# A recorded and list-scheduled instruction order in a two-layer GDN/GLA decoder trunk

## The chip, the core and the metric

The kernel runs on one core of a Trainium2 chip. TensorE (PE in the profile) multiplies matrices into PSUM, VectorE (DVE), ScalarE (ACT) and GpSimd (POOL) do the elementwise work, and SyncE (SP) starts most transfers between HBM and the on-chip memory SBUF. Each engine works through its own list of instructions in a fixed order; an instruction waits at the head of its list until the semaphores that it names are high enough, and nothing behind it on that engine can pass. The metric is device time in microseconds (us) of one execution.

## What is computed

Two layers over 2048 tokens of width 1024, in float32. Layer 0 is a gated DeltaNet (GDN) with 8 heads, layer 1 is gated linear attention (GLA) with 4 heads; head keys have 128 channels, values 256.

```python
def reference(x, ...):
    for i in range(2):
        y = gdn_mixer(x, ...) if i == 0 else gla_mixer(x, ...)
        x = layer_norm(DEEP_ALPHA * x + y, ln_g[i], ln_b[i])
    return x
# a mixer: p = x @ w_in -> q, k, v, gate (and per-token decay logits)
# GDN: short causal conv + silu on q, k, v; S_t = exp(g) S (I - beta k k^T) + beta v k^T; o = S q
# GLA: S_t = diag(exp(gk_t)) S + k^T v; o = q S
# both: o * rms(o) * norm_w * silu(gate), then @ w_out
```

## The kernel before

The work is cut into 48 units: a unit is one head (`h`) of one group of 512 tokens (`gi`) in one layer (`kind`). `PHASES` sets the order of the groups: GDN 0, GDN 1, GLA 0, GDN 2, GLA 1, GDN 3, GLA 2, GLA 3; a GDN group has 8 units, a GLA group 4. Inside a unit there are four threads of work:

- `gemms`: three input projections (`kq`, `val`, `gate`). Each runs over 8 chunks of 128 rows of the weight. A chunk of the weight is loaded to `wraw`, rounded by ACT to `wh`, and POOL writes the rest `wl = wraw - wh`; the input is split likewise into `xh` and `xl` (`load_x`, ACT and DVE). A float32 product is then three passes in the faster type fp32r (`mm3`: hi*hi, hi*lo, lo*hi). The sums stand in the PSUM banks `psg` (three of them).
- `preps`: the within-chunk matrices. For GDN (`gdn_prep`) this holds a triangular inverse: its diagonal blocks `X` go to HBM (`blk`) and come back replicated (`Arep`), then DVE solves 15 steps in turn (`Xt`, `X`), and PE and DVE widen the inverse (`Tm`, `U`, `W2`) to `Uf`, written over `D1`.
- `chains`: the recurrence over 4 chunks of 128 tokens. In GDN a chunk is `kq`*`S` (PE, into `psh`), `Rt` (DVE), `Uf`*`Rt` (PE), `wt` (ACT copy), `kd`*`wt` (PE), `S` (DVE): three round trips from PE and back, one `psh` bank. Then `og` is transposed and split to `oth`, `otl`.
- `outs`: the output projection, 8 pairs (token tile, half of the width) of a unit, each a *group* of 6 matmuls into `pso`, of which there is one bank, and one DVE instruction that adds it to `y` (`y<-pso,z,y`). The bank is free for the next group when that instruction is done. After the last head of a group comes the LayerNorm.

All 48 units are unrolled. The order on the engines comes about in two steps. The threads are Python generators; `Plan` keeps a rough clock of the engines (`COST`), and `plan.run` always continues the first thread whose operands should be there (chains, preps, outs, gemms, in that order). `O_GAP` keeps two output groups 7050 ns apart on that clock, `Y_WAIT` holds the first `y` load back, `W.load` starts weight loads `W_BUFS` = 9 chunks ahead. The order in which instructions are emitted is their urgency for the scheduler of the language's tile layer, which then sets the order on each engine by its own model, and places the tiles in their buffers. Every recorded operation carries line L121, so the rows below are told apart by their tiles.

## Time and profile before

| | |
|---|---|
| time, median of 3 runs | 3254.07 us (3253.61 to 3254.88) |
| span of the profiled execution | 3246.0 us, 55989 instructions |
| busy: PE, DVE, ACT, POOL | 3064.1, 2466.0, 1565.6, 1127.2 us |
| DMA over the span | 299.83 MB, mean 92 GB/s |
| median less span | 8.07 us |

The span runs from the first to the last instruction in the profile; the median of the runs is 8.07 us more, which lies around it. A row of a timeline reads: start, duration, engine, line, operation, output<-inputs, sizes, count, and in brackets the idle time before it and what ended it. A matmul's record is longer than the distance to the next one, since matmuls overlap in the array: a row of many merged matmuls gives the true distance. In float32 a matmul is two records, and in fp32r one.

### The profile page before, as it was taken

The page shows a single profiled execution, that of the slowest core. Times are in us where ns is not written, and L with a number is a line of the kernel's source. Part 1 is how long each engine was busy: PE and PEld are TensorE (multiplying, and loading weights), DVE is VectorE, ACT ScalarE, POOL GpSimd, SP SyncE. Part 2 cuts the span into 40 slices and gives each one's busy share as a digit, 9 for nine tenths or more (in the row PEclk, how much of TensorE's full clock was granted, in tenths as well). Part 3 has the DMA queues.
Part 4 walks back from the last instruction along what each step waited for, and adds up shares of the span by engine and source line. Part 5 has one row for each costly group of instructions (what it writes and reads, how often), then busy time and mean ns, then how long its engine had stood idle before and what let it go on. Part 6 is the DMA issues. An engine that isn't in the chain of part 4 may idle for free.

```text
span 3246.0 us, 55989 instructions
## 1 busy us (share of the span) xinstructions
PE 3064.1 (94%) x18430; PEld 2601.6 (80%) x18430; DVE 2466.0 (76%) x6345; ACT 1565.6 (48%) x4099; POOL 1127.2 (35%) x1506
## 2 busy tenths in 40 slices
PE   8899999989999999998999999999899999899997
PEld 7688778768888888877887888978778878798885
DVE  7677788787877687688778768677877786866677
ACT  5445444445444456444444545553444454465542
POOL 5333333333233234334233324432433322433341
PEclk9899999999999999999999999999999999999998
DMA  6222223242222315324222322532422232243231
GB/s 179 63 77 74 78 73 98 82 147 76 74 78 78 101 53 153 109 79 127 80 79 82 92 73 67 153 98 78 136 77 74 82 94 69 78 137 97 66 125 59
DMA packets 311604, 299.83 MB, mean 92 GB/s; under 512 B 40544, under 2 KB 253792, under 8 KB 311312
## 3 DMA queue, kind: packets, MB, share of 16 engines
q1 hardware_dynamic: 285200, 278.42, 30.0%
q10 hardware_dynamic: 26112, 17.83, 1.9%
q8 instruction: 145, 2.38, 0.3%
q14 instruction: 147, 1.20, 0.1%
HBM read 269.86 MB, written 26.28 MB: 91 GB/s over the span
## 4 chain that ended last, share of the span: by engine, by line
PE 47%; DVE 20%; DMA 7%; issue 2%; ACT 2%; POOL 0%; SPq 0%; DVEq 0%; ACTq 0%; POOLq 0%
PE psg L121 24%; PE psc L121 10%; PE pso L121 10%; DMA Arep<-blk 5%; PE psh L121 4%; DVE X L121 3%; DVE D L121 2%; DVE y L121 2%; DVE acc L121 2%; DVE Xt L121 2%; DVE lntmp L121 1%; DMA blk<-X 1%; DVE z L121 1%; DVE lnrs L121 1%; DVE lnst L121 1%
## 5 line engine op out<-in xcount | busy, mean ns | idle before, releaser
L121 POOL TENSOR_TENSOR wl<-wraw,wh 128x256 fp32r<-128x256 f32 x1152 | 950.0, 843 | 1349.7 <-ACT wh L121 1207.9
L121 ACT CAST wh<-wraw 128x256 fp32r<-128x256 f32 x1152 | 444.6, 405 | 373.9 <-PE psg L121 229.2
L121 PE MATMUL psg<-wh,xh 128*128 128x256 f32 (+1 forms) x2048 | 609.5, 298 | 12.8 <-ACT acc L121 6.1
L121 PE MATMUL psg<-wl,xh 128*128 128x256 f32 (+1 forms) x2048 | 586.4, 286 | 2.7 <-POOL wl L121 2.5
L121 PE MATMUL psg<-wh,xl 128*128 128x256 f32 (+1 forms) x2048 | 585.7, 286 | 0.0
L121 PE MATMUL psg<-xh,wh 128*128 128x512 f32 x1280 | 525.6, 411 | 2.9 <-DVE vt L121 1.3
L121 PE MATMUL psg<-xl,wh 128*128 128x512 f32 x1280 | 518.8, 405 | 0.6 <-DVE xl L121 0.6
L121 PE MATMUL psg<-xh,wl 128*128 128x512 f32 x1280 | 514.8, 402 | 0.1
L121 PEld LDWEIGHTS psg<-wh,xh 128*128 128x128 f32 x2048 | 392.6, 192 | 30.4 <-ACT acc L121 6.9
L121 PEld LDWEIGHTS psg<-wl,xh 128*128 128x128 f32 x2048 | 393.3, 192 | 16.5 <-POOL wl L121 3.8
L121 PEld LDWEIGHTS psg<-wh,xl 128*128 128x128 f32 x2048 | 392.9, 192 | 1.0
L121 PE MATMUL pso<-woh,oth 128*128 128x512 f32 x736 | 326.3, 443 | 61.7 <-DVE y L121 55.7
L121 DVE SCALAR_TENSOR_TENSOR acc<-pb,taps,acc 128x512 f32<-128x512 f32 x384 | 330.1, 862 | 44.4 <-ACT acc L121 39.1
L121 DVE SCALAR_TENSOR_TENSOR y<-pso,z,y 128x512 f32<-128x512 f32 x368 | 273.6, 743 | 111.7 <-PE pso L121 109.2
L121 PE MATMUL pso<-woh,otl 128*128 128x512 f32 x736 | 304.8, 414 | 12.9 <-DVE otl L121 11.5
L121 PE MATMUL pso<-wol,oth 128*128 128x512 f32 x736 | 298.6, 406 | 0.0
L121 PEld LDWEIGHTS psg<-xh,wh 128*128 128x128 f32 x1280 | 243.9, 191 | 56.1 <-DVE sg L121 3.2
L121 PEld LDWEIGHTS psg<-xh,wl 128*128 128x128 f32 x1280 | 242.7, 190 | 54.7 <-POOL wl L121 1.0
L121 PEld LDWEIGHTS psg<-xl,wh 128*128 128x128 f32 x1280 | 243.4, 190 | 53.4 <-DVE xl L121 2.5
L121 ACT ACTIVATE junk<-psc 128x128 bf16<-128x128 f32 (+1 forms) x448 | 144.2, 322 | 185.4 <-PE psc L121 150.8
L121 PEld LDWEIGHTS pso<-woh,oth 128*128 128x128 f32 x736 | 140.2, 190 | 100.9 <-DVE y L121 72.0
L121 DVE TENSOR_TENSOR Xt<-Arep,X 128x60 f32<-128x60 f32 (+14 forms) x480 | 131.9, 275 | 84.7 <-DMA Arep<-blk 76.6
(192 smaller groups left out, 5459.0 us busy)
## 6 DMA issues: line engine op xcount, KB each, us to landing
wraw<-in_w_in SPq DMA_DIRECT2D x1152, 128.0 KB, 2.3
woraw<-in_w_out SPq DMA_DIRECT2D x192, 256.0 KB, 3.6
Arep<-blk SPq DMA_DIRECT2D x32, 512.0 KB
woraw<-in_xT SPq DMA_DIRECT2D x32, 256.0 KB, 3.2
y<-in_x SPq DMA_DIRECT2D x16, 512.0 KB, 4.3
Gb<-gcT ACTq DMA_DIRECT2D x32, 256.0 KB, 3.0
x<-y SPq DMA_DIRECT2D x32, 256.0 KB, 2.1
x2T<-th ACTq DMA_DIRECT2D x32, 256.0 KB, 4.4
```

The source lines that it names most:

```text
L121: ins = op(*args, **kw)
```

## The change

The threads become plain functions, called for one unit after the other; nothing is emitted then. A `Recorder` notes each operation with its operands (`View`s of buffers that are not yet chosen), the operations that it depends on, a cost, and a rank: chains 0, preps 1, outs 2, gemms 3. `place` then runs a list schedule over five engines (DVE, ACT, POOL, PE, SP): the engine that can start soonest takes, of the operations whose operands and buffers are there, the one with the lowest rank, and within a rank the earlier one. It also gives a new tile the buffer that came free first. An operation that needs a new tile is held back while its unit is more than `HORIZON` = 2 units ahead of the oldest unit whose chain isn't finished. `emit` writes the operations in the order found, and ties each to the operation before it on its engine with an edge that carries no wait, so the tile layer's scheduler can't reorder them. The multiset of instructions is the same: 15921 matmuls, 1646 transfers on SP, and so on for each engine.

```diff
-class Plan:
-    def note(self, key, aps):
...
-COST = {"v": (110, 1.04), "s": (110, 0.84), "g": (90, 2.35), "w": 800, "t": 200, "d": 450, "dw": 2000}
+class Recorder:
+    def cost(self, op, dst, every):
+        if key == "t":
...
+                op.cost = mov / 2.25 + 4.5
+            op.lag = 210
+        elif key == "d":
+            op.cost, op.lag = 430, 1700 + size / 170
...
+        elif key == "v":
+            took = (150 if psum else 160) + 1.04 * n
+            if op.name == "scalar_tensor_tensor":
+                took += 55
+            if len(every) > 2 and not psum and n > 64:
+                took *= 1.12
+            op.cost, op.lag = took - 80, 80 + LAG
+        elif key == "s":
+            took = (165 if psum else 210) + 0.833 * n
...
+        else:
+            took = 140 + 2.8 * n if len(every) > 2 else 300 + n
+            op.cost, op.lag = took - 40, 40 + LAG
+    def place(self):
...
+        while len(placed) < len(self.ops):
+            best = None
+            for e in clock:
...
+                s = clock[e] if avail[e] else pending[e][0][0] if pending[e] else None
+                if s is not None and (best is None or s < best[0]):
+                    best = s, e
...
+            op = self.ops[heapq.heappop(avail[e])[1]]
...
+            for t in op.fresh:
+                slot = min(free[t.tag])
+                free[t.tag].remove(slot)
+                t.slot = slot[1]
...
+    def emit(self, tc):
...
+        for op in self.place():
+            tc.keep_in_program_order(op.call(*[real(a) for a in op.args], **{k: real(a) for k, a in op.kw.items()}))
...
     def load_x(u, kc):
-        raw = T("woraw", [P, TG], WO_RAW_BUFS)
...
+        raw = T("xraw", [P, TG], 2)
...
     def load_gb(u):
...
-                t = T("woraw", [P, 512], WO_RAW_BUFS)
+                t = T("gb", [P, 512], 4)
...
-    plan.run(chains(), preps(), outs(), gemms(), start=(0.0, 0.0, 1.0, 0.0))
+    for u in units:
+        rec.unit = u.at
+        gemms(u)
+        preps(u)
+        chains(u)
+        outs(u)
+    rec.emit(tc)
...
-O_GAP = 7050
-Y_WAIT = 20000
+R_CHAIN, R_PREP, R_OUT, R_GEMM = range(4)
+HORIZON = 2
...
-    nc = bacc.Bacc("TRN2", target_bir_lowering=False, num_devices=1)
+    nc = bacc.Bacc("TRN2", target_bir_lowering=False, num_devices=1, dynamic_dma_scratch_size=1024)
```

Input chunks get two raw buffers of their own (`xraw`); before, they shared the four of `woraw` with the output weights.

Three places show how the order moves. The first is the head of SP's list, the first loads of the program. In before, weight chunks (`wraw`) and input chunks (`in_xT`) alternate:

```order
L121 DMA wraw_113<-in_w_in 128x2x128
L121 DMA woraw_119<-in_xT 128x512
L121 DMA wraw_125<-in_w_in 128x2x128
L121 DMA woraw_131<-in_xT 128x512
L121 DMA wraw_137<-in_w_in 128x2x128
```

The changed kernel's list begins with:

```order
L345 DMA y_232<-in_x 128x1024
L345 DMA y_233<-in_x 128x1024
L345 DMA y_234<-in_x 128x1024
L345 DMA y_235<-in_x 128x1024
L345 DMA woraw_236<-in_w_out 128x512
L345 DMA woraw_237<-in_w_out 128x512
L345 DMA woraw_238<-in_w_out 128x512
L345 DMA woraw_239<-in_w_out 128x512
L345 DMA taps_65<-in_conv 128x128
L345 DMA nalog_66<-in_a_log 128x8
L345 DMA dtb_67<-in_dt_bias 128x8
L345 DMA cst_63<-in_consts 128x1408
```

After these and `nw` come the first input and weight chunks: outputs' loads (rank 2) now stand ahead of the projections' (rank 3). From the ninth load on, each waits in the program for an older one to land.

The second place is DVE's list at the end of the 15-step solve of the 13th GDN unit. In before, the output sum `y` stands behind the solve, two conv sums (`acc`), `qd`, `Tm` and `U`:

```order
L121 SCALAR_TENSOR_TENSOR acc_10617<-pb_10613,taps_65,acc_10617 128x512
L121 TENSOR_TENSOR X_10394<-X_10394,Xt_10395 128x4
L121 TENSOR_TENSOR qd_11034<-kq_10463,Gb_11019 128x512
L121 TENSOR_TENSOR Tm_10384<-X_10394,cst_63 128x512
L121 SCALAR_TENSOR_TENSOR acc_10617<-pb_10613,taps_65,acc_10617 128x512
L121 STREAM_TRANSPOSE U_10385<-Tm_10384 128x512
L121 SCALAR_TENSOR_TENSOR y_8198<-pso_10537,z_10445,y_8198 128x512
```

In the changed kernel's solve of the same unit:

```order
L345 TENSOR_TENSOR Xt_213<-Arep_212,X_210 128x4x14
L345 SCALAR_TENSOR_TENSOR y_233<-pso_248,z_225,y_233 128x512
L345 TENSOR_TENSOR X_210<-X_210,Xt_213 128x4x14
L345 SCALAR_TENSOR_TENSOR wol_245<-woraw_237,nw_0_68,woh_241 128x512
L345 TENSOR_TENSOR Xt_213<-Arep_212,X_210 128x4x13
L345 SCALAR_TENSOR_TENSOR vt_162<-th_105,psg_109 128x512
L345 TENSOR_TENSOR X_210<-X_210,Xt_213 128x4x13
L345 SCALAR_TENSOR_TENSOR y_234<-pso_248,z_225,y_234 128x512
```

The output sums now stand between the steps of the solve, each next to short instructions, and no conv sum is there.

The third place is PE's list in the recurrence of a GDN unit, from `psh<-Rt` (the product with the inverse) to `psh<-wt` (the product that updates the state). In before:

```order
L121 MATMUL psh_8776<-Rt_8778,D_1953_7845 128x256
L121 MATMUL psc_8798<-kq_8094 128x256
L121 MATMUL pso_8787<-woh_8218,oth_8107 128x512
L121 MATMUL psh_8776<-wt_8789,kd_7863 128x256
L121 MATMUL psc_8791<-wt_8789,D_1954_7846 128x256
```

In the changed kernel:

```order
L345 MATMUL psh_217<-Rt_219,D_0_184 128x256
L345 MATMUL psg_107<-xh_114,wl_150 128x512
L345 MATMUL psg_107<-xh_115,wh_142 128x512
L345 MATMUL psg_107<-xl_123,wh_142 128x512
L345 MATMUL psg_107<-xh_115,wl_151 128x512
L345 MATMUL psg_107<-xh_116,wh_143 128x512
L345 MATMUL psg_107<-xl_124,wh_143 128x512
L345 MATMUL psh_217<-wt_221,kd_196 128x256
L345 MATMUL psc_173<-wt_221,D_0_186 128x256
```

Single matmuls of a projection now stand in the round trip, six where there were two others.

## The prediction

> **What bounds the kernel now.** I read the page's busy shares first, then the chain of waits for the true distance of matmuls, then the waits of TensorE, then single stretches. The page:

> ```profile
> span 3246.0 us, 55989 instructions
> PE 3064.1 (94%) x18430; PEld 2601.6 (80%) x18430; DVE 2466.0 (76%) x6345; ACT 1565.6 (48%) x4099; POOL 1127.2 (35%) x1506
> ```

> TensorE (PE) shows work in 94% of the span, and 3246 - 3064 = 182 us without. But its records overlap, so 3064 isn't its work. The chain in order of time merges matmuls that follow without a wait, and gives their distance:

> ```profile
> 3023.97 0.69 PE pso L121 x3
> 3032.88 4.25 PE psg L121 x36
> 3031.99 0.89 PE psc L121 x8
> 3178.29 0.86 PE psc L121 x4
> ```

> An fp32r matmul 512 wide takes 0.69/3 = 0.23 us, one 256 wide 4.25/36 = 0.118. A float32 record takes 0.111 (128 wide) or 0.215 (256 wide); a product is two of these, a transpose one. A GDN unit has 144 matmuls 512 wide (48 each for kq, val and the output: 33.1 us), 96 for the gate (11.3), 24 float32 products 256 wide (20 in the recurrence, 4 in the preparation: 10.3), 24 transposes and 8 products 128 wide (4.4), and small products for the inverse (about 2): 61.1 us. The period of such units is read from one transfer that each makes once:

> ```profile
> 822.78 0.60 SPq L121 DMA_DIRECT2D Arep<-blk  x1
> 1087.11 0.61 SPq L121 DMA_DIRECT2D Arep<-blk  x1
> ```

> Three more stand between these two, so four periods are 264.3 us, 66.1 each. TensorE is thus the bound: 5.0 us (8%) of a period isn't its work. In the stretch of the next row its idle time is 264.33 - 257.01 = 7.3 us, 1.8 a unit, at full clock; the other 3.1 are waits too short to show between overlapping records.

> ```profile
> 822.78:1087.11 264.33, 257.01 (x1519) 214.43 (x1518) 210.13 (x542) 128.53 (x355) 90.46 (x132) 1.00 0.30 85
> 1087.11:1400.91 313.80, 302.62 (x1940) 264.93 (x1939) 227.06 (x563) 163.40 (x401) 115.84 (x140) 0.99 0.35 99
> ```

> The second row holds four GLA units and one GDN unit. By the same count a GLA unit is 57 us (96 wide matmuls 22.1, 192 for value and gate 22.7, 12 float32 products 256 wide 5.2, the rest about 7), so 289 of 313.8 us are work. Over 32 + 16 units the work is 1955 + 912 = 2867 us, with the LayerNorm's transposes and the group heads about 2890. So some 355 us of the span are not TensorE's work, and only waiting and clock can be won, since the change removes no instruction.

> Who is waited for:

> ```profile
> PE pso L121 <- DVE y L121: 60.8, 36, 5.4
> PE pso L121 <- DVE otl L121: 11.5, 10, 3.2
> PE psh L121 <- DVE S L121: 9.8, 5, 3.1
> PE psc L121 <- DVE W L121: 9.2, 4, 3.1
> ```

> The output bank is first: 60.8 us in 36 waits. One of them, on TensorE and then on VectorE:

> ```profile
> 903.85 0.39 PE L121 MATMUL pso<-woh,otl 128*128 128x512 f32 x1
> 911.85 0.50 PE L121 MATMUL pso<-woh,oth 128*128 128x512 f32 x1 [1.36 <-DVE y L121]
> ```
> ```profile
> 910.46 0.70 DVE L121 STREAM_TRANSPOSE U<-Tm 128x512 f32<-128x512 f32 x1
> 911.08 0.71 DVE L121 SCALAR_TENSOR_TENSOR y<-pso,z,y 128x512 f32<-128x512 f32 x1
> ```

> The group ended at 904.2 and its sum started at 911.08, 6.8 us later, though VectorE had worked on projections' sums meanwhile: it stood too far back in the list (the second place in the change's section). Spacing the groups on TensorE didn't help.

> **The change part by part.** No work is added or removed; the parts are orders.

> *Output sums.* They now stand in the solve, behind instructions of 0.2 us, by rank ahead of all projection sums. In return the groups come close: between one group's last matmul and the next group's first, before puts at least 4.25 us of TensorE work in 263 of 399 cases, the changed kernel in 44 of 367 (counted on the order, at the distances above). What a group needs, where the sum comes at once:

> ```profile
> 3195.43 0.40 PE L121 MATMUL pso<-woh,otl 128*128 128x512 f32 x1
> 3196.68 0.50 PE L121 MATMUL pso<-woh,oth 128*128 128x512 f32 x1 [0.42 <-DVE y L121]
> ```

> That is 1.25 us from last matmul to next first. So the wait of 60.8 us can go to nothing (if the sum is always next) or grow (below, as a rival). I take 0.4 of it as left, 24 us, since a tight place has no reserve: -37.

> *Round trips.* At the third place TensorE has 0.43 + 6 x 0.23 = 1.8 us from `psh<-Rt` to `psh<-wt`; before has 0.43 + 0.43 + 0.23 = 1.09. What such a step needs:

> ```profile
> 879.58 0.48 DVE L121 SCALAR_TENSOR_TENSOR S<-S,eg,psh 128x256 f32<-128x256 f32 x1
> ```
> ```profile
> 878.88 0.67 PE L121 MATMUL psh<-wt,kd 128*128 128x256 f32 x2
> 880.12 0.70 PE L121 MATMUL psh<-S,kq 128*128 128x256 f32 x2
> ```

> 1.24 us from start to start, with a VectorE that took the state at once. Of the 320 steps inside GDN's recurrences, 110 have less than that in matmuls in before, 45 in the changed kernel (counted on the order). That goes for the short waits (3.1 us a unit) and the visible ones on `psh`, `psc`, `psg`. The first 150 us hold 24 us of idle time, three stretches of 50 us:

> ```profile
> 0.00:50.00 50.00, 44.55 (x215) 34.89 (x216) 32.52 (x59) 26.05 (x65) 30.54 (x44) 1.00 0.69 207
> 50.00:100.00 50.00, 40.00 (x208) 34.08 (x207) 41.06 (x94) 23.61 (x66) 22.49 (x32) 0.93 0.44 116
> 100.00:150.00 50.00, 41.14 (x213) 31.49 (x212) 31.87 (x95) 18.73 (x62) 10.71 (x18) 0.86 0.19 49
> ```

> Visible idle outside the output wait, these 24 us and the last 46 us (22 idle, below) is 182 - 61 - 46 = 75 us; I take half: -38 (0 to -75). Of the short waits, about 3.1 x 48 = 149 us with GLA's, I take a quarter: -37 (0 to -149). I don't take more, because the new order is exact to single matmuls and so has a place for each delay to show.

> *Durations that the planner assumes.* They decide how true its order is. Its formulas give 737 ns for `y`, 857 for `wl`, 423 for `wh`, 775 for `xl`. The trace:

> ```profile
> L121 POOL TENSOR_TENSOR wl<-wraw,wh 128x256 fp32r<-128x256 f32 x1152 | 950.0, 843 | 1349.7 <-ACT wh L121 1207.9
> L121 ACT CAST wh<-wraw 128x256 fp32r<-128x256 f32 x1152 | 444.6, 405 | 373.9 <-PE psg L121 229.2
> L121 DVE SCALAR_TENSOR_TENSOR y<-pso,z,y 128x512 f32<-128x512 f32 x368 | 273.6, 743 | 111.7 <-PE pso L121 109.2
> L121 DVE TENSOR_TENSOR xl<-woraw,xh 128x512 fp32r<-128x512 f32 x64 | 59.0, 939 | 14.2 <-ACT xh L121 13.9
> ```

> Three are right within 5%, the fourth is 20% too short.

> *The start.* Eight loads now stand ahead of the first input chunk: 4 x 512 + 4 x 256 KB = 3.1 MB, and `cst` with 704 KB. The rows of before, and the rates in 40 slices of the first 60 us:

> ```profile
> GB/s 0 164 301 190 305 368 269 235 297 111 39 354 330 36 126 153 164 153 410 407 409 365 194 12 11 52 188 142 207 204 111 227 287 221 166 229 279 169 147 217
> ```
> ```profile
> 4.44 0.62 ACT L121 CAST xh<-woraw 128x512 fp32r<-128x512 f32 x1 [1.00 <-DMA woraw<-in_xT]
> 5.53 1.06 PE L121 MATMUL psg<-xh,wh 128*128 128x512 f32 x2
> ```

> At the best rate, 410 GB/s, 3.1 to 3.9 MB take 7.7 to 9.4 us. So the first projection starts 8 to 9 us later, near 14 us. TensorE then idles some 7 us after its warm-up matmuls, and idle costs clock:

> ```profile
> 105.00:110.00 5.00, 3.97 (x16) 3.29 (x14) 3.52 (x6) 0.81 (x2) 0.00 (x0) 0.50 0.00 0
> 110.00:115.00 5.00, 5.00 (x50) 3.87 (x48) 1.40 (x2) 0.51 (x2) 0.00 (x0) 0.81 0.00 0
> ```

> After an idle stretch at 104 us the granted clock was 0.50 for 5 us and 0.81 for 5 more: 2.5 + 0.95 = 3.4 us lost. By that row I add 3. [...] Start: +12 (0, if the recurrence of the first unit hides it, to +15).

> *Input chunks at the seven group borders.* Two raw buffers serve 8 chunks; a pair takes a load (3.2 us to landing), a cast (0.62) and a subtraction (0.94), near 4.8 us, so 8 chunks need some 19 us where the first gate needs 12. The order fills 15 to 22 us of other matmuls and this gate's into that stretch, so I cost it at nothing; without that cover it is 7 us a border, 49 in all.

> *The end.* The last 46 us hold 22 us of idle time, in sums, LayerNorm and stores that depend on each other; I cost it at nothing.

> ```profile
> 3200.00:3246.00 46.00, 24.14 (x108) 18.94 (x106) 40.98 (x113) 9.80 (x15) 9.40 (x6) 0.81 0.19 69
> ```

> Sum: -37 - 38 - 37 + 12 = -100, so a span of 3146 us. The runs' median, 3254.07, is 8 us above the span, which lies around it: 3154.

> **Rivals.** *The output bank becomes the wait (slower).* Some 320 groups have no reserve, and VectorE is busy 76% of the time. If two groups in three find a conv sum of 0.862 us in front, as its group's row has it,

> ```profile
> L121 DVE SCALAR_TENSOR_TENSOR acc<-pb,taps,acc 128x512 f32<-128x512 f32 x384 | 330.1, 862 | 44.4 <-ACT acc L121 39.1
> ```

> that is 213 x 0.862 = 184 us in place of 60.8: +123, less 75 for the other two gains, plus 12: +60, so 3314. It turns slower where 0.862 x groups passes 60.8 + 75 - 12 = 124 us: from about 145 groups, 45 in 100. For it: VectorE's durations vary, and a fixed order can't step aside. A step of the solve took 0.20 us and the next but one 0.62, while POOL was in a row of `wl`:

> ```profile
> 898.73 0.20 DVE L121 TENSOR_TENSOR Xt<-Arep,X 128x44 f32<-128x44 f32 x1
> 899.78 0.62 DVE L121 TENSOR_TENSOR Xt<-Arep,X 128x40 f32<-128x40 f32 x1
> ```

> Against it: rank puts the sum ahead of conv sums. [...]

> *Input chunks starve TensorE at the borders (a smaller gain).* Without cover, +49: 3203. For it: two buffers where before shared four, and a subtraction that takes longer than planned; against: other work is placed there.

> *The order hardly matters.* If waits only move, as queues on VectorE stay as long, the start remains: 3254 to 3266.

> **How the numbers follow.** A measurement of this kernel tells about 0.2% (6.5 us) from no change. Chances: the forecast 0.60, the starved borders 0.10, no matter 0.05 (0.04 of it within 0.2%), the output bank and its kin 0.25. Faster 0.70, same 0.04, slower 0.26. If all waits that I halve or quarter went, the sum would be -61 - 75 - 149 + 0 = -285, 2969; I think that far end unlikely for an order with no reserve, and set the lower end where three quarters of the visible waits and six tenths of the short ones go and the start costs nothing: -46 - 56 - 89 = -191, 3063. The upper end, 3290, takes in about half of the slower rival.

> **What would show it.** Right: TensorE's idle time falls from 182 to near 110 us, `pso<-y` to about 24, a GDN period from 66.1 to about 64.5, the first projection near 14 us with a clock under 1 behind it. The output rival would show as a wait `pso<-y` over 120 us; starved borders as waits on `xh` or `xl` of 5 us and more. I am wrong if the periods stay at 66, or if they come down below 63, where the short waits would have gone nearly all.

## Result, and the profile after

The changed kernel takes 3502.24 us (median of 4 runs, 3501.01 to 3505.12), the kernel before 3254.48 (3253.61 to 3257.15) beside it: a ratio of 1.0762, with a 95% interval of 1.0747 to 1.0778. It is 7.6% slower, 248 us. The forecast was 3154, and its upper end 3290. The 8 us that the forecast put between the span and the median mostly parted two executions: where time and span of one execution are on record, they are 1.7 to 3.0 us apart.

The page of the changed kernel, its first lines:

```profile
span 3498.9 us, 55902 instructions
PE 3146.7 (90%) x18430; PEld 2636.5 (75%) x18430; DVE 2548.6 (73%) x6345; ACT 1566.9 (45%) x4099; POOL 1096.2 (31%) x1506
```

TensorE shows no work for 3498.9 - 3146.7 = 352 us, where it was 182. Span and granted clock, of before and then of the changed kernel:

```profile
core 0: 3246.0 us, clock 0.983
```
```profile
core 0: 3498.9 us, clock 0.964
```

A clock of 0.983 over 3246 us withholds 55 us of full clock, one of 0.964 over 3498.9 us 126 us (an upper bound of what it costs, since some of it falls into idle time). With the prediction's 2890 us of work, what is left for waits too short to show is 3246 - 2890 - 182 - 55 = 119 us in before, and 131 in the changed kernel. So the 253 us of span between them are about 170 of visible waits, up to 71 of clock and, as what is left over, 12 of short waits.

Who is waited for, from the waits of TensorE (total us, times, longest):

```profile
PE pso L345 <- DVE y L345: 58.6, 47, 3.6
PE psc L345 <- DVE U L345: 42.4, 21, 3.3
PE psc L345 <- DVE og L345: 32.3, 29, 3.0
PE psg L345 <- DVE acc L345: 21.6, 9, 7.7
PE psg L345 <- DVE sg L345: 20.5, 12, 2.6
PE psh L345 <- DVE S L345: 16.5, 13, 2.1
```

The output bank, which was the largest wait in before (60.8 us), is as it was. What is new is spread over everything that VectorE makes: the inverse (`U`), the gated output (`og`), conv sums, gates, the state. Added up over all rows, TensorE's visible waits for VectorE rose from 127 to 254 us, for ScalarE from 27 to 54 (13 of them before the first projection), for GpSimd from 2.5 to 17. So no one wait took the place of another; VectorE comes late everywhere. It costs in every part of the program: the loads of `Arep` of the 8th, 16th and 32nd GDN unit start 29, 80 and 201 us later than in before. Between the loads of `Arep` for the same two units as in the prediction (the 12th and the 16th),

```profile
878.69 0.61 SPq L345 DMA_DIRECT2D Arep<-blk  x1
1167.15 0.60 SPq L345 DMA_DIRECT2D Arep<-blk  x1
```

there are 288.5 us, 72.1 a unit where it was 66.1.

One of the 21 waits for `U` shows the way in which it comes. GpSimd, VectorE and TensorE at the end of a 15-step solve (some of VectorE's rows left out):

```profile
361.64 0.74 POOL L345 TENSOR_TENSOR wl<-wraw,wh 128x256 fp32r<-128x256 f32 x1 [17.39 <-ACT wh L345]
363.18 5.43 POOL L345 TENSOR_TENSOR wl<-wraw,wh 128x256 fp32r<-128x256 f32 x7 [0.79 <-ACT wh L345]
```
```profile
361.23 0.18 DVE L345 TENSOR_TENSOR Xt<-Arep,X 128x20 f32<-128x20 f32 x1
361.44 0.18 DVE L345 TENSOR_TENSOR X<-X,Xt 128x20 f32<-128x20 f32 x1
361.66 0.75 DVE L345 TENSOR_TENSOR Xt<-Arep,X 128x16 f32<-128x16 f32 x1
363.29 1.24 DVE L345 SCALAR_TENSOR_TENSOR wol<-woraw,nw,woh 128x512 fp32r<-128x512 f32 x1
364.45 0.71 DVE L345 TENSOR_TENSOR X<-X,Xt 128x12 f32<-128x12 f32 x1
365.78 0.41 DVE L345 SCALAR_TENSOR_TENSOR sg<-th,psg 128x256 f32<-128x256 f32 x1
366.60 0.66 DVE L345 TENSOR_TENSOR Xt<-Arep,X 128x4 f32<-128x4 f32 x1
367.29 0.66 DVE L345 TENSOR_TENSOR X<-X,Xt 128x4 f32<-128x4 f32 x1
369.41 0.70 DVE L345 STREAM_TRANSPOSE U<-Tm 128x512 f32<-128x512 f32 x1
```
```profile
370.16 1.57 PE L345 MATMUL psc<-U,D 128*128 128x128 f32 x8 [2.64 <-DVE U L345]
```

A step of the solve takes 0.18 us until GpSimd starts on `wl` at 361.64, 20 ns ahead of the step at 361.66, which then takes 0.75. During GpSimd's row of seven four of the six steps take 0.66 to 0.71 us, though they handle 4 to 12 elements a partition in place of 20; of the other two, one took 0.45 and one, which started 20 ns behind the row's start, its usual 0.16. The gate at 365.78 reads PSUM and takes its usual 0.41. TensorE stands for 2.64 us at the first matmul that reads `U`. GpSimd itself had waited 17.39 us for ScalarE's `wh`, so its work came in one piece.

The theory after this reading, called A: the planner gives TensorE's dependent matmuls the place where by its clock the operand is just ready, with a small reserve (its constant LAG, 60 ns); VectorE instructions that start while GpSimd subtracts end later than the planner knows (0.66 to 0.75 us for 0.18 in five of the steps above); the list can't step aside, so TensorE waits (2.64 us here), and long waits cost clock (0.964 over the run, where it was 0.983). Rival B: the pins (the edges that tie each operation to the one before it) are the cause, since the tile layer's scheduler may no longer reorder. Rival C: the planned order itself is too long (ranks, group borders, first loads).

### The profile page after: what moved, and what is told of

Its sections match the earlier page's. It is cut to its first block, busy times and chain, and to the rows that moved or that the text cites. A ratio compares the mean times of both kernels' runs of the same rounds, so it can differ in the third digit from the quotient of the medians.

```text
span 3498.9 us, 55902 instructions
## 1 busy us (share of the span) xinstructions
PE 3146.7 (90%) x18430; PEld 2636.5 (75%) x18430; DVE 2548.6 (73%) x6345; ACT 1566.9 (45%) x4099; POOL 1096.2 (31%) x1506
## 4 chain that ended last, share of the span: by engine, by line
PE 47%; DVE 20%; DMA 5%; ACT 3%; issue 3%; POOL 0%; SPq 0%; ACTq 0%; DVEq 0%; POOLq 0%
PE psg L345 24%; PE psc L345 11%; PE pso L345 9%; PE psh L345 3%; DMA Arep<-blk 3%; DVE acc L345 2%; DVE y L345 2%; DVE X L345 2%; DVE Xt L345 2%; DVE D L345 1%; DVE ztmp L345 1%; DVE z L345 1%; ACT junk L345 1%; DVE wol L345 1%; DMA woraw<-in_w_out 1%
## 5 line engine op out<-in xcount | busy, mean ns | idle before, releaser
L345 POOL TENSOR_TENSOR wl<-wraw,wh 128x256 fp32r<-128x256 f32 x1152 | 932.0, 826 | 2059.6 <-ACT wh L345 1717.9
L345 PE MATMUL psg<-wl,xh 128*128 128x256 f32 (+1 forms) x2048 | 601.4, 295 | 2.2 <-POOL wl L345 2.2
L345 PE MATMUL psg<-wh,xl 128*128 128x256 f32 (+1 forms) x2048 | 593.1, 294 | 0.0
L345 PE MATMUL psg<-xh,wh 128*128 128x512 f32 x1280 | 535.7, 419 | 37.2 <-ACT wh L345 15.7
L345 PE MATMUL psg<-xh,wl 128*128 128x512 f32 x1280 | 536.3, 421 | 5.8 <-POOL wl L345 5.7
L345 PE MATMUL psg<-xl,wh 128*128 128x512 f32 x1280 | 530.1, 415 | 0.2
L345 PEld LDWEIGHTS psg<-wh,xh 128*128 128x128 f32 x2048 | 399.2, 195 | 44.4 <-DVE vt L345 18.1
L345 PEld LDWEIGHTS psg<-wl,xh 128*128 128x128 f32 x2048 | 400.0, 195 | 11.5 <-POOL wl L345 2.8
L345 PE MATMUL pso<-woh,oth 128*128 128x512 f32 x736 | 314.3, 427 | 59.8 <-DVE y L345 58.6
L345 ACT ACTIVATE th<-psg 128x256 f32<-128x256 f32 (+1 forms) x256 | 109.7, 436 | 360.6 <-PE psg L345 290.0
```

Source lines behind the costliest of these rows:

```text
L345: tc.keep_in_program_order(op.call(*[real(a) for a in op.args], **{k: real(a) for k, a in op.kw.items()}))
```

## The experiments

### Zeros in place of the subtraction, in both kernels

In the changed kernel the order stays; only the instruction is another (`ZERO[0]` is GpSimd's memset):

```diff
+            args, call = [real(a) for a in op.args], op.call
+            if op.key == "g" and op.name == "tensor_tensor" and op.args[0].of.tag == "wl":
+                args, call = [args[0].bitcast(F32), 0.0], ZERO[0]
...
```

In the kernel before `split(...)` of a weight chunk becomes `s.copy(h, raw)` and a memset of `l`.

> The changed kernel with its order untouched, but GpSimd writes zeros to `wl` in place of the subtraction, so the low half of the weights is left out of the computation; GpSimd reads nothing there. Theory A (no reserve, and VectorE's instructions that start while GpSimd is in a `wl` run until its end): VectorE's mean durations fall to those of its quick instructions, about 290 us less VectorE time, TensorE's idle time falls well below 352 us, and the time to 3150-3250. Rival B (the pins keep the tile layer's scheduler from stepping aside): little changes, 3400-3500. Rival C (the planned order itself is too long: ranks, group borders, first loads): 3400-3500, and 200 us or more above the same edit of the kernel before.

> The kernel before with the same edit: GpSimd writes zeros to `wl`, the low half of the weights is left out. Theory A: it gains too, but less than the changed kernel, since TensorE comes later to what VectorE makes: 3030-3110 (150-220 us less than before), so that of the 248 us between the two kernels 80-130 are left. Rival B: the distance between the two kernels stays near 250. Rival C: it stays at 200 or more.

Measured, one run each: 3251.75 us for the changed kernel (250 less) and 3122.52 for the one before (130 less). Both times miss what was expected, the first by 2 us (3150 to 3250), the second by 13 (3030 to 3110): the kernel before depends less on GpSimd than A had it. VectorE's busy time fell from 2548.6 to 2260.3 us in the changed kernel, about the 290 us expected. The two groups of a solve's steps, in the changed kernel and then with zeros:

```profile
L345 DVE TENSOR_TENSOR Xt<-Arep,X 128x60 f32<-128x60 f32 (+14 forms) x480 | 137.8, 287 | 63.2 <-DMA Arep<-blk 51.4 <-POOL wl L345 1.0
L345 DVE TENSOR_TENSOR X<-X,Xt 128x60 f32<-128x60 f32 (+14 forms) x480 | 134.4, 280 | 11.3 <-DVE Xt L345 0.2
```
```profile
L348 DVE TENSOR_TENSOR Xt<-Arep,X 128x60 f32<-128x60 f32 (+14 forms) x480 | 91.7, 191 | 73.3 <-DMA Arep<-blk 62.7
L348 DVE TENSOR_TENSOR X<-X,Xt 128x60 f32<-128x60 f32 (+14 forms) x480 | 91.5, 191 | 11.3 <-DVE Xt L348 0.2
```

A step falls from 284 to 191 ns; over the 30 steps of a solve that is 2.8 us, the size of the waits for `U`. They are nearly gone:

```profile
PE pso L348 <- DVE y L348: 41.0, 39, 3.1
PE psc L348 <- DVE U L348: 3.9, 6, 1.0
```

In the kernel before with zeros the output bank stands at:

```profile
PE pso L121 <- DVE y L121: 13.2, 16, 3.3
```

So with quick instructions in both, the output bank costs the changed kernel 28 us more than the kernel before; the near-equal 58.6 and 60.8 us above hid that its groups stand too close.

Rivals B and C in their plain form expected 3400 or more for the changed kernel. Of the distance between the two kernels 129 us are left, within A's 80 to 130; this rest isn't from the subtraction of `wl`. The memset is also shorter than the subtraction (313 ns where that takes 826) and reads nothing, so `wl` is ready and `wraw` free sooner: the pair of kernels doesn't part that from the shorter VectorE instructions. It can't be the main part, since TensorE's visible waits for GpSimd were 17 us in all in the changed kernel, and none of its visible waits was for a transfer.

### The planner's reserve: LAG 0, 200, 400

```diff
-LAG = 60
+LAG = 200
```

> One constant of the planner: LAG, the time that it adds to the result of every VectorE, ScalarE and GpSimd instruction, is 200 ns in place of 60, so that dependents are planned later and other work stands between. Theory A: 3300-3390, with fewer waits of TensorE and a higher granted clock. Rival B: 3480-3520, the pins are the same. Rival C: 3490-3560, since a plan with longer latencies is no shorter.

> LAG is 0 in place of 60: the planner hands results over with no reserve at all. Theory A (reserve): slower still than the changed kernel's 3502, 3530-3600, with more waits of TensorE. Against it (the 200 ns helped by chance, as any other order would, or because a plan with other latencies differs in its ranks): anywhere between 3330 and 3500.

> LAG is 400. Theory A has a best value: with more reserve than an instruction is stretched by (half a us at most, and rarely), the chains of dependent instructions get longer in the plan than they are, TensorE runs out of planned work, and the time rises again: 3350-3450. If reserve only ever helps: 3300 or less.

Measured: LAG 0, 3565.9 us (one run); 60, 3502.24; 200, 3328.74 (3325.28 to 3330.23), a ratio to the kernel before of 1.0234 (1.0219 to 1.0249); 400, 3506.95 (one run). The waits of TensorE for `U` with LAG 0, and with LAG 200:

```profile
PE psc L345 <- DVE U L345: 82.8, 23, 6.3
```
```profile
PE pso L345 <- DVE y L345: 34.3, 43, 2.3
PE psg L345 <- DVE acc L345: 24.8, 13, 3.7
PE psc L345 <- DVE U L345: 4.5, 7, 1.1
```

82.8, 42.4 and 4.5 us for a LAG of 0, 60 and 200 ns: thirty dependent steps of a solve get 30 x 140 ns = 4.2 us more in the plan, more than the 2.8 us by which they are late. Rivals B and C expected no gain. LAG isn't the whole reserve of a hand-over to TensorE: the plan adds 100 ns more there, and in the trace TensorE starts 56 ns behind VectorE's record (median of 143 waits), so by the plan's durations 44 ns were to spare with LAG 0, 104 with 60 and 244 with 200. The stretching itself is nearly the same: counted on the trace, the time of VectorE's instructions above the quick quarter of their own kind is some 360 us in the changed kernel and 345 with LAG 200 (307 in before). What changes is whether TensorE stands there.

With LAG 400 the time rises again, as expected, but by more than the 3350 to 3450 named. Another wait has become the largest:

```profile
PE psg L345 <- DVE acc L345: 122.8, 30, 7.5
PE psc L345 <- DVE D L345: 30.2, 30, 3.7
```

The wait for `U` isn't among the large ones; the conv sums, lowest in rank, are late in its place. One of these waits:

```profile
2001.80 0.39 PE L345 MATMUL pso<-woh,otl 128*128 128x512 f32 x1
2006.46 0.44 PE L345 MATMUL psg<-cst,acc 128*128 128x128 f32 x2 [4.26 <-DVE acc L345]
```

It recurs about once a GDN unit, 27 times, most often with 4.2 to 5.3 us, mostly where the unit's load of `Arep` is near. In this one VectorE worked through a preparation ahead of the conv sum, at its quick durations, so the wait stands in the plan and isn't made by a stretch. That is a loss of the kind that the expectation named (plans longer than the chains are), though its bound on a stretch, half a us, was too small: the step shown above got 0.57 us longer. Why the plan does so at 400 and not at 200 was not followed. It also shows that another LAG is another order, which can gain or lose much by itself. Part of the 174 us of LAG 200 may be such luck; no other order with the same LAG was tried. Against luck alone stand the waits for `U`, which fall as LAG rises, LAG 0, slower as expected and outside the 3330 to 3500 of the chance rival, and the next experiment.

### Reserve without GpSimd's reads

LAG 200 together with the zeros.

> LAG 200 and zeros in place of the `wl` subtraction (the low half of the weights is left out). Theory A in its strict form (the reserve is needed for VectorE's instructions that GpSimd stretches): with those gone the reserve has little left to do, 3200-3270, at most 50 us under the same edit with LAG 60 (3251.75), though it brought 174 us with GpSimd at work. Against it (the planner's hand-overs are too short in any case): the two gains add up, 3080-3150.

Measured, one run: 3210.5 us. The four cases side by side:

| | `wl` subtracted | zeros | difference |
|---|---|---|---|
| LAG 60 | 3502.24 | 3251.75 | 250 |
| LAG 200 | 3328.74 | 3210.5 | 118 |
| difference | 174 | 41 | |
| kernel before | 3252.17 | 3122.52 | 130 |

Within each of the rows LAG 60 and LAG 200 the order is the same, and only GpSimd's instruction differs. The reserve is worth 174 us with GpSimd subtracting and 41 with zeros: most of what it brings is that the stretched instructions cost less. With LAG 200 the planned order is as sensitive to GpSimd as the kernel before (118 and 130 us). The 41 us lie under the 50 that A in its strict form allowed, and 3210.5 within its 3200 to 3270.

### Without the pins

```diff
-            tc.keep_in_program_order(op.call(*[real(a) for a in op.args], **{k: real(a) for k, a in op.kw.items()}))
+            op.call(*[real(a) for a in op.args], **{k: real(a) for k, a in op.kw.items()})
```

> The changed kernel without the edges that tie each operation to the one before it on its engine: the tile layer's scheduler may reorder. Theory A: 3430-3560, no gain, since that scheduler doesn't know VectorE's stretched instructions either. Rival B: 3330 or less, most of the loss gone. Rival C: 3430-3560 as well, as the emitted order stays the urgency.

Measured: 3504.03 us (3495.11 to 3508.05), ratio to the kernel before 1.0768 (1.0746 to 1.0789). Taking the pins away gains nothing. The order that the tile layer's scheduler then makes waits in other places, for `U` only 11.4 us, and is no better:

```profile
PE pso L345 <- DVE y L345: 71.9, 69, 3.7
PE psc L345 <- DVE og L345: 39.0, 20, 3.4
```

Rival B falls.

### What the planner doesn't know besides

The program puts two engines that only read the same PSUM bank one after the other: 281 such waits between VectorE and ScalarE stand in the changed kernel on `psc`, such as `og` behind `junk`, and the planner didn't know of them. LAG 200 with this and two more edits:

```diff
-                if meet and (write or owrite) and other is not op:
+                if meet and (write or owrite or (t.psum and key != okey)) and other is not op:
...
+            if op.key == "d" and op.prio[0] == R_OUT:
+                ready = max(ready, 40000.0)
...
-        raw = T("xraw", [P, TG], 2)
+        raw = T("xraw", [P, TG], 3)
```

> LAG 200, and three edits of what the planner doesn't know or do: two engines that read the same PSUM bank are put one after the other in the plan, as they are in the program; input chunks have three raw buffers in place of two; loads for the outputs start 40 us into the plan, behind those of the first projection. Theory A says that after the reserve only such smaller things are left between 3329 and the kernel before: 3270-3310. If the rest is reserve too: 3320-3340.

Measured: 3290.08 us (3287.0 to 3293.35), ratio 1.0116 (1.0099 to 1.0133): 39 us less than LAG 200 alone, as A expected. One part can be read off, the first projection, with LAG 200 alone and in this one:

```profile
18.43 1.22 PE L345 MATMUL psg<-xh,wh 128*128 128x512 f32 x2 [12.57 <-ACT wh L345]
```
```profile
10.04 1.22 PE L347 MATMUL psg<-xh,wh 128*128 128x512 f32 x2 [3.95 <-ACT xh L347]
```

That is at most 8 of the 39 us. The edits weren't tried one by one. The 38 us to the kernel before, and the 88 us between LAG 200 and before with zeros in both (3210.5 and 3122.52), stay open. More than half of the 88 arises in the first third of the program: the load of `Arep` of the 16th GDN unit starts at 1080.55 us with LAG 200 and zeros, at 1035.01 in before with zeros, and 13 of these 46 us stand ahead of the first projection (18.56 and 5.52 us).

### Less work for GpSimd, whole computation

If GpSimd's subtractions cost the kernel before 130 us, it should gain from fewer of them. Weights are the same for all four token groups of a layer, so each chunk is rounded and subtracted once, and both halves are kept in HBM:

```diff
...
+                if key in kept:
+                    for t, part in zip((h, l), kept[key]):
+                        sync.dma_start(t[:, :n].bitcast(F32), part[:, :n])
+                else:
...
+                    kept[key] = [T(f"k{t}_{len(kept)}", [P, 272], 1, F32, dr) for t in "hl"]
+                    for t, part in zip((h, l), kept[key]):
+                        acts.dma_start(part[:, :n], t[:, :n].bitcast(F32))
```

> The kernel before, whole computation, with one edit: each weight chunk is rounded and subtracted only in the first token group of its layer, both halves are written to HBM, and the other three groups load them from there, so GpSimd's `wl` instructions fall from 1152 to 288. If VectorE's stretched instructions cost the kernel before what the zeros gave back (130 us in 1152 instructions), three quarters of it come back less what the stores take: 3140-3190. If the zeros helped by something else (loads that wait less, TensorE's data): 3220 or more.

Measured: 3273.44 us (3271.06 to 3280.59), ratio 1.0072 (1.0057 to 1.0087): a miss. VectorE's time fell to 2273.3 us, but the first token group lost it again. The first 600 us of before, and of this kernel (length, PE busy and count, then PEld, DVE, ACT, POOL, clock, DMA share, GB/s):

```profile
0.00:600.00 600.00, 562.65 (x3201) 463.26 (x3201) 455.74 (x1150) 284.71 (x802) 210.16 (x311) 0.98 0.33 91
```
```profile
0.00:600.00 600.00, 524.36 (x2878) 429.21 (x2879) 396.75 (x1040) 247.39 (x701) 169.27 (x270) 0.94 0.57 170
```

The stores of `wl` stand in ScalarE's list, where they wait for GpSimd with ScalarE's other work behind them: ScalarE worked 247.39 of these 600 us, where it was 284.71. So they were moved to SP, four chunks late:

```diff
-                    for t, part in zip((h, l), kept[key]):
-                        acts.dma_start(part[:, :n], t[:, :n].bitcast(F32))
+                    late.append((kept[key], (h, l), n))
+                if len(late) > 4 or late and late[-1][0] is not kept[key]:
+                    parts, tiles, m = late.pop(0)
+                    for t, part in zip(tiles, parts):
+                        sync.dma_start(part[:, :m], t[:, :m].bitcast(F32))
```

> As before_keep (whole computation), but the stores of the rounded weights stand on SP, four chunks behind their `wl`, and not on ScalarE, where they made ScalarE wait for GpSimd in the first token group. If only that place cost before_keep its gain: the first 600 us lose no more than 15 us against the kernel before, and the whole takes 3170-3220. If the loads of twice the bytes cost the rest: 3240-3290.

Measured: 3188.01 us (3184.56 to 3191.73), ratio 0.9808 (0.9791 to 0.9824), inside the expected 3170 to 3220: 1.9% faster than the kernel before, with all of the computation, and the fastest whole version of this study. The edit also takes three quarters of the roundings (`wh`) off ScalarE, whose busy time falls from 1565.6 to 1278.1 us; what GpSimd's part alone is worth was not tried. Its first 600 us, 43 matmuls (some 8 us) behind those of before, and its page:

```profile
0.00:600.00 600.00, 559.85 (x3158) 460.00 (x3159) 426.65 (x1132) 267.58 (x742) 174.25 (x278) 0.97 0.60 181
```
```profile
span 3189.7 us, 55398 instructions
PE 3047.8 (96%) x18430; PEld 2592.2 (81%) x18430; DVE 2269.8 (71%) x6345; ACT 1278.1 (40%) x3235; POOL 402.2 (13%) x642
```

The same edit was put on the kernel of the three edits, with all transfers on SP, in the planner's order.

> after_more with the weights kept in HBM (whole computation), all transfers on SP, placed by the planner. Theory A: GpSimd's `wl` falls to a quarter, so VectorE runs nearer to the planner's durations: 3190-3260. If the transfers' landing times, which the planner only guesses, take the place of the stretched instructions: 3290 or more.

Measured: 3292.58 us (3282.51 to 3296.87), ratio 1.0128 (1.0108 to 1.0148), no gain over 3290.08. It is outside A's 3190 to 3260 and where the rival, landing times of transfers, had it. This speaks against A as I had put it, or at least shows what it leaves out: VectorE's time came down as in the kernel before, to 2273.3 us, and the time didn't. The waits of TensorE:

```profile
PE pso L347 <- DVE y L347: 67.2, 34, 5.2
PE psg L347 <- DVE acc L347: 18.1, 12, 5.9
PE psg L347 <- ACT xh L347: 16.1, 15, 4.2
PE psg L347 <- DMA wh<-kh: 10.3, 5, 4.0
```

Waits for the loads are there (`wh<-kh`), but they are too small to be all of it. It is another order, as each edit of the recorded work gives another, and its largest wait is again the output bank. What cost it the gain stays open.

## Why the prediction was wrong

- **The step that failed is the one under "Round trips" and "Output sums": room counted in matmuls was taken for reserve.** I counted how many matmuls stand between a step's start and its use, and set that against the time of a round trip in which VectorE took the work at once (1.24 us). The planner had done the same, with 104 ns to spare. What decides is when VectorE really delivers. Counted on trace and program, 3296 matmuls in before and 3452 in the changed kernel wait for another engine; in before 20% of them started less than 0.4 us behind the end of the record that they wait for, in the changed kernel 35%. More round trips had room for their usual length, and fewer had room for a stretched one. So the visible idle time outside the output bank, of which I halved the larger part (-38), rose from 182 - 61 = 121 to 352 - 59 = 293 us (+172), and the waits too short to show, which I cut by a quarter (-37), from 119 to 131 (+12).
- **The output sums** were taken from 60.8 to 24 us. They stayed, 58.6 us in 47 waits. LAG 200 gives 34.3, and the zeros 41.0: rank alone didn't get every sum started at once. In one of these waits (1.97 us, to 1685.28) the group's last matmul ended at 1682.03 and the sum started at 1684.48, behind four steps of the solve that took 0.64 to 0.67 us beside a row of GpSimd's `wl` (the first of them was running at 1682.03) and one that took 0.21. With zeros in both the kernel before has 13.2, so the close groups cost something even without stretched instructions.
- **The slower rival** had the right mechanism (VectorE's durations vary, a fixed order can't step aside) and quoted a stretched step, but gave it one place, the output bank, which didn't grow. It was worth 3314; the place was every hand-over of VectorE. "I don't take more, because the new order is exact to single matmuls and so has a place for each delay to show" limited a gain where it should have been priced as a loss. The row was there: the steps of a solve took 0.20 and 0.62 us. Times 30 steps and 32 solves it can be priced; I compared the planner's formulas with mean durations of long instructions only (`y`, `wl`, `wh`, `xl`) and called three of four right, while the mean of an `Xt` step, 275 ns in before and 191 without GpSimd's subtraction, was not looked at. The planner's formula gives 164 to 222 ns for it, the quick step.
- **Clock.** I costed it at the start only, 3 us. Over the run it is 126 us of full clock withheld against 55. In the records the granted clock is at half for 254 us in 48 stretches, in before for 116 us in 24, all but one in each a whole multiple of 3.41 us long. All half-clock stretches of a run begin on one grid of 3.41 us, and in the changed kernel each of the 48 follows a window of the grid in which TensorE showed no work for 1.86 us or more, while of the 902 other windows at full clock one held 1.91 and the rest at most 1.83 (in before 1.90 or more in the 24, at most 1.75 in 892). So in these two traces a window at full clock with some 1.9 us without work was, but for that one, paid for twice: half-clock time followed it, 3.41 us or more. Over whole runs: with LAG 200 the clock is 0.974, with zeros 0.985.
- **The start** was forecast at +12 us, with the first projection near 14 us. It came at 18.84 us, 13.3 later than in before, and the first 50 us ran at a clock of 0.86:

```profile
18.84 1.22 PE L345 MATMUL psg<-xh,wh 128*128 128x512 f32 x2 [12.97 <-ACT wh L345]
```
```profile
0.00:50.00 50.00, 32.44 (x158) 25.76 (x159) 20.92 (x40) 21.95 (x50) 17.39 (x29) 0.86 0.60 185
650.00:700.00 50.00, 37.88 (x173) 29.47 (x173) 46.43 (x105) 26.98 (x66) 28.46 (x33) 0.86 0.56 174
1500.00:1550.00 50.00, 35.69 (x143) 26.00 (x143) 38.92 (x97) 24.69 (x70) 34.10 (x39) 0.93 0.50 156
```

- **The borders** were costed at nothing. The last two rows are two of them, with 12 and 14 us idle in 50; in before no such 50 us between 150 and 3100 us hold more than 7.8. The rival named waits on `xh` or `xl` of 5 us for them; the longest wait on `xh` is 1.2 us, so it wasn't the input chunks as I had it. Among the longest waits in these two rows are those for GpSimd's `y` of the LayerNorm (3.6 us) and for the next group's decay logits `lgz` (4.8).

Where theory A stands: that the reserve and GpSimd's subtractions belong together is shown by the four cases; that the pins aren't it is shown. Of the 248 us, 119 are gone when GpSimd writes zeros in place of subtracting (129 are left between the two kernels), and the larger reserve takes 41 of these 129. The last 88 are the planned order's own, shown in size and not in cause, so A explains about two thirds of the loss, as far as LAG 200 isn't also a lucky order.

## What to carry to other kernels

A schedule from a planner is as good as its worst-known duration: before you trust counted room, compare each chain's mean duration with its quick one in the trace, above all for chains of many short dependent steps, and ask how much later than planned the last step may come. Give the hand-overs a reserve, and measure its size, since here a LAG of 200 ns was worth 174 us and one of 400 nothing; each value gives another order, so look at the waits too. GpSimd's subtractions of two SBUF tiles were paid for by VectorE here (384 ns more for each of 314 tensor_tensor instructions, below): rounding and subtracting once and loading the result again was worth 1.9% in the kernel before, provided that the stores didn't stand in a busy engine's list, and nothing in the planned order.
